# State space phase tables computed for two stages at once, one per half of the partitions

## The chip, the cores and the metric

The kernel runs on one core of a Trainium2 chip. The metric is device time in microseconds of one execution of the whole program, the median of several runs. The program is one decoder layer on 1024 tokens of width 1024, in 32-bit floats.

## The reference, cut to what matters

One layer adds to its input the merged output of three causal token mixers (an attention with forget gates, a diagonal state space, a gated linear recurrence), then a cross attention over 256 memory rows, then a SwiGLU block. The change lies in the state space mixer, with 32 groups of 16 channels and 64 complex states per group:

```
abar = exp(dt * a)                    # a complex, one per group and state
h[t] = abar * h[t-1] + bbar u[t]      # complex, per group and state
y[t] = Re(c h[t]) + d_skip * u[t]
out  = gelu(y) * sigmoid(gelu(y) w_glu + b_glu)
```

The kernel computes the recurrence over chunks of eight tokens: within a chunk by a Toeplitz matrix, from chunk to chunk (128 of them) by a scan. The scan runs on real numbers: each chunk's drive is turned by the angle that the state has moved through up to that chunk, scanned with the magnitude of abar to the eighth power, and turned back. The cosine and sine of these angles, for 128 chunks, are the phases. They depend on the group and the state alone.

## The kernel before, in words

All activations lie transposed, channels on the 128 partitions and tokens along the columns. A 32-bit weight or activation is split into a rounded part and the rest (`wh` and `wl`, `xh` and `xl`): ScalarE writes the first and VectorE the second, by subtraction, and each product is three TensorE matmuls of 128x512 (`pj` groups in PSUM).

The state space mixer is done in eight stages of four groups. A partition pair p and p+64 holds the real and the imaginary part of state p, so the parameters stand twice, once in each half of the partitions, and a sign column `sgn` (-1 below, +1 above) makes the sine's sign differ between the halves. `s5_params` prepares the tables, all with 32 groups along the columns: powers of abar, and two small tables of turned angles, `eb` (16 fine steps) and `ear`, `eai` (8 coarse steps), seeded by GpSimd copies and VectorE scalings and filled by complex products on VectorE.

`s5_main` runs eleven rounds, one stage a round at each of four lags. Round i calls `s5_prep` of stage i (GpSimd products into the tile `s5x`, loads of `s5u`), `s5_out` of stage i-3 (the matmuls `s5y`, which read `kcs`, then the gelu on VectorE and ScalarE in turns, then a store), `s5_prep2` of stage i-1 (the phases, a transposition `s5g`, small matmuls `s5k`, copies on ScalarE, eight DMAs into `toep`), and `s5_body` of stage i-2 (the matmuls `s5d`, multiplication by the phases, four scans, multiplication back, the result in `kcs`). So a stage's phases are computed in the round before its body. They are six VectorE instructions of 128x512: from `ear`, `eai` and `eb` by broadcasting, into the tile `s5e` (cosines in its first 512 columns, signed sines in the second), with a scratch half of `s5tm` between. `toep` and `kcs` have two halves, used in turns by the stage's parity.

Between the stages' calls `pump` places other work for TensorE: the projections of the remaining inputs and gates (`gz`, the value projection `vs` with its weights `w_v`, attention queries and keys `qs`). The Tile framework takes all this in program order with a priority for each instruction, which `ahead` raises (60 for the stages, 60 for weight splits), and fixes each engine's order of instructions at build time by priority and by its own estimate of when an instruction's inputs are ready. On the chip each engine goes through its order and waits on semaphores. Tiles come from one pool of 50 buffers of 128x1024 and 8 PSUM banks; an instruction that first writes a buffer waits for the last readers of what lay there. All DMAs are issued from SyncE's queue.

The names that matter below: `s5_params` (line 898), `s5_prep` (1090), `s5_prep2` (1123), `s5_body` (1171), `s5_out` (1199), `s5_main` (1226). Line 244 is the helper of all two-input element operations, 241 that of ScalarE's activations, 226 that of matmuls, 260 that of scalar operations.

Of the kernel before, what the change touches and what calls it, by code (L numbers as in the profile page):

```python
# [13 lines left out]
AF = mybir.ActivationFunctionType  # L14
# [5 lines left out]
P = 128  # L20
# [50 lines left out]
HG_LAT = 5.0  # L71
FOXL_W = 10.0
FOXL_T = 8.0
EPS = 1e-6
NEG = -1e30
HG_LEVELS = (1, 2, 4, 8, 16)
# [116 lines left out]
class Trunk:  # L193
# [704 lines left out]
    def s5_params(self):  # L898
        nc = self.nc
        V, G = nc.vector, nc.gpsimd  # L900
# [14 lines left out]
        ADD, MUL, SUB = ALU.add, ALU.mult, ALU.subtract  # L915
# [18 lines left out]
        k, r, dt, f2 = tiny(), tiny(), tiny(), tiny()  # L934
# [28 lines left out]
        ang = self.u("s5ang").rearrange("p (q m g) -> p q m g", q=4, m=8)  # L963
# [20 lines left out]
        s, v = ang[:, 2, 0], ang[:, 3, 0]  # L984
        t = tiny()
        yield
        nr, ni, ar1, c = tiny(), tiny(), tiny(), tiny()
# [24 lines left out]
        cx = self.u("s5cx").rearrange("p (a g h) -> p a g h", a=2, h=16)  # L1012
# [23 lines left out]
        tmv = tm.rearrange("p a g h -> p a (g h)")  # L1036
        for n in (1, 2, 4):
            tmp = [tmv[:, i, 0:32 * n].rearrange("p (g k) -> p g k", k=n) for i in range(2)]
# [6 lines left out]
        rv = self.u("s5rv")  # L1045
# [5 lines left out]
        yield  # L1051


        eb = self.u("s5eb").rearrange("p (a g k) -> p a g k", a=2, k=16)
        ear = rv[:, 256:512].rearrange("p (g k) -> p g k", k=8)
        eai = rv[:, 512:768].rearrange("p (g k) -> p g k", k=8)
        for m, j in ((1, 0), (2, 1), (3, 3), (4, 7), (5, 15)):
            G.tensor_copy(out=eb[:, 0, :, j], in_=ang[:, 1, m])
            self.ts(eb[:, 1, :, j], ang[:, 2, m], self.sgn, -1.0, MUL, MUL)
        G.memset(ear[:, :, 0], 1.0)  # L1060
        G.memset(eai[:, :, 0], 0.0)
        for m, j in ((5, 1), (6, 2), (7, 4)):
            G.tensor_copy(out=ear[:, :, j], in_=ang[:, 1, m])
            self.ts(eai[:, :, j], ang[:, 2, m], self.sgn, -1.0, MUL, MUL)

        def fill(tr, ti, first, n, base):
            tmp = [tmv[:, i, 0:32 * n].rearrange("p (g k) -> p g k", k=n) for i in range(2)]
            self.cmul(tr[:, :, base + 1:base + 1 + n], ti[:, :, base + 1:base + 1 + n],
                      tr[:, :, first:first + n], ti[:, :, first:first + n],
                      tr[:, :, base:base + 1].to_broadcast([P, 32, n]),  # L1070
                      ti[:, :, base:base + 1].to_broadcast([P, 32, n]), V, tmp)

        for n in (1, 3, 7):
            fill(eb[:, 0], eb[:, 1], 0, n, n)
# [4 lines left out]
        tz, kz = self.u("toep"), self.u("kcs")  # L1079
# [40 lines left out]
        self.add(Z1, Z1, T, G)  # L1120
        d.update(U=U, ut=ut, xt=xt, X=X, Z1=Z1)

    def s5_prep2(self, o):
        nc = self.nc
        g0 = 4 * o
        gs = slice(g0, g0 + 4)
        d = self.s5o[o]
        ut, xt, X, Z1 = (d[k] for k in ("ut", "xt", "X", "Z1"))
        cx = self.cx

        def bh(t):
            return t[:, gs].unsqueeze(3).to_broadcast([P, 4, 8, 16])

        def bk(t):
            return t[:, gs].unsqueeze(2).to_broadcast([P, 4, 8, 16])


        et = self.u("s5e")
        dt_ = self.u("s5dd")
        CO = et[:, 0:512].rearrange("p (g a j) -> p g a j", g=4, a=8)  # L1140
        SI = et[:, 512:1024].rearrange("p (g a j) -> p g a j", g=4, a=8)
        tq = self.s5t[:, 1].rearrange("p (g a j) -> p g a j", g=4, a=8)
        ar, ai = bh(self.ear), bh(self.eai)
        br, bi = bk(self.eb[:, 0]), bk(self.eb[:, 1])
        self.mul(CO, ar, br)
        self.mul(tq, ai, bi)
        self.sub(CO, CO, tq)
        self.mul(SI, ar, bi)
        self.mul(tq, ai, br)
        self.add(SI, SI, tq)  # L1150

        gp = self.psm("s5g")
        for g in range(4):
            self.tp(gp[:, 128 * g:128 * g + 128], X[:, g].rearrange("p s h -> p (s h)"))

        kp = self.psm("s5k")
        for g in range(4):
            x0 = X[:, g, 7]
            self.mm(kp[0:16, 128 * g:128 * g + 16], x0, cx[:, 0, g0 + g])
            self.mm(kp[0:16, 128 * g + 16:128 * g + 128], x0, Z1[:, g, 0:7].rearrange("p k h -> p (k h)"))  # L1160
        G1 = xt[:, 0:512]
        self.act(G1, gp, AF.Copy)
        kt = ut[0:16, 512:1024]
        self.act(kt, kp[0:16], AF.Copy)
        tz = self.toep[o % 2]
        ktv = kt.rearrange("p (g c) -> p g c", g=4)
        for s in range(8):
            nc.sync.dma_start(out=tz[16 * s:16 * s + 16, :, 16 * s:128], in_=ktv[:, :, 0:128 - 16 * s])
        d.update(et=et, dt=dt_, G1=G1.rearrange("p (g c) -> p g c", g=4), tz=tz)

    def s5_body(self, o):

        d = self.s5o[o]
        U, et, dt_, G1 = (d[k] for k in ("U", "et", "dt", "G1"))
        COf, SIf = et[:, 0:512], et[:, 512:1024]
        d1 = self.psm("s5d1")
        for g in range(4):
            self.mm(d1[:, 128 * g:128 * g + 128], G1[:, g], U[:, g])
        r1, r2 = dt_[:, 0:512], dt_[:, 512:1024]
        lo, hi = slice(0, 64), slice(64, 128)  # L1180
        self.mul(r1, d1, COf)
        self.mul(r2[lo], d1[hi], SIf[hi])
        self.mul(r2[hi], d1[lo], SIf[lo])
        self.sub(r1, r1, r2)
        for g in range(4):
            c = slice(128 * g, 128 * g + 128)
            a = self.r8[:, 4 * o + g:4 * o + g + 1].to_broadcast([P, 128])
            self.nc.vector.tensor_tensor_scan(out=r1[:, c], data0=a, data1=r1[:, c], initial=0.0,
                                              op0=ALU.mult, op1=ALU.add)
        kc = self.kcs[o % 2]  # L1190
        kv = r1.rearrange("p (g c) -> p g c", g=4)
        cv, sv = COf.rearrange("p (g c) -> p g c", g=4), SIf.rearrange("p (g c) -> p g c", g=4)
        m = r2.rearrange("p (g c) -> p g c", g=4)[:, :, 1:128]
        self.mul(kc[:, :, 1:128], kv[:, :, 0:127], cv[:, :, 0:127])
        for a, b in ((lo, hi), (hi, lo)):
            self.mul(m[a], kv[b, :, 0:127], sv[b, :, 0:127])
        self.add(kc[:, :, 1:128], kc[:, :, 1:128], m)

    def s5_out(self, o):

        nc = self.nc
        g0 = 4 * o
        d = self.s5o.pop(o)
        U, ut, Z1, tz = (d[k] for k in ("U", "ut", "Z1", "tz"))
        kc = self.kcs[o % 2]
        yp = self.psm("s5y")
        for g in range(4):
            c = yp[:, 128 * g:128 * g + 128]
# [16 lines left out]

    def s5_main(self):

        self.s5o = {}
        for o in range(11):
            for lag, stage in ((0, self.s5_prep), (3, self.s5_out), (1, self.s5_prep2), (2, self.s5_body)):  # L1230
                if 0 <= o - lag < 8:
                    stage(o - lag)
                    yield S5_W[lag] * (S5_END if o > 8 else S5_BEG if o < 2 else 1.0)
            if o == FOX_AT:
                self.need("ff")
                self.fox_alloc()
# [1083 lines left out]
```

## Time and profile before

| | |
|---|---|
| device time, median of 3 runs | 2147.52 us (2146.33 to 2148.11) |
| the profiled execution, device time | 2145.49 us |
| its span, first to last instruction | 2143.7 us |
| TensorE matmuls busy | 2073.8 us, 97% of the span |
| VectorE busy | 1525.9 us, 71% |
| ScalarE busy | 814.1 us, 38% |
| GpSimd busy | 610.7 us, 28% |

The state space stages lie between about 107 and 322 us of the span. In a profile PE is TensorE, DVE is VectorE, ACT is ScalarE, POOL is GpSimd and SP is SyncE. A row's releaser (after `<-`) is what the idle time ended with. Durations of neighbouring instructions overlap a little, so their sum can be over the elapsed time.

### The profile page before, as it was taken

How to read it: one execution, taken by the hardware profiler on the slowest of the kernel's cores; microseconds unless marked ns; L12 is line 12 of the kernel's file. 1: busy time of each engine (PE TensorE's matmuls, PEld its weight loads, DVE VectorE, ACT ScalarE, POOL GpSimd, SP SyncE). 2: the span in 40 equal slices, each digit the busy share in tenths (PEclk: the TensorE clock that was granted, in tenths of full speed). 3: DMA queues.
4: the chain of work that ended last, by engine and by line, in shares of the span. 5: the costliest groups of instructions: out<-in, count | busy, mean ns of one | idle time of the engine just before them, and what ended most of it. 6: DMA issues, size and time to landing. Idle time of an engine off the chain costs nothing.

```text
span 2143.7 us, 26772 instructions
## 1 busy us (share of the span) xinstructions
PE 2073.8 (97%) x10044; PEld 1701.3 (79%) x10044; DVE 1525.9 (71%) x2221; ACT 814.1 (38%) x1268; POOL 610.7 (28%) x495
## 2 busy tenths in 40 slices
PE   8998999999999999999999999999999999989899
PEld 5887776776788888887888888878788888878677
DVE  8888898889845576536665576756878787866764
ACT  4113355556421222216334455534433333334231
POOL 4281204455531111000603000011432232425740
PEclk9999999999999999999999999999999999999999
DMA  4332120110210121124434533243222232269783
GB/s 162 137 103 75 51 86 21 40 50 30 79 54 30 50 69 55 59 98 171 159 102 144 197 90 108 79 165 125 92 97 102 99 123 98 99 228 356 267 292 132
DMA packets 102610, 245.18 MB, mean 114 GB/s; under 512 B 15816, under 2 KB 32200, under 8 KB 102480
## 3 DMA queue, kind: packets, MB, share of 16 engines
q1 hardware_dynamic: 102480, 243.46, 32.9%
q8 instruction: 79, 1.29, 0.2%
q14 instruction: 51, 0.42, 0.1%
HBM read 184.83 MB, written 57.41 MB: 113 GB/s over the span
## 4 chain that ended last, share of the span: by engine, by line
PE 65%; DVE 4%; issue 1%; DMA 1%; ACT 1%; POOL 1%; SPq 0%; DVEq 0%; POOLq 0%; ACTq 0%
PE pj L226 32%; PE fp L226 26%; PE hs L226 2%; PE xo L226 1%; DVE wc L244 1%; PE rs L226 1%; PE xs L226 1%; DVE hl L244 1%; PE ho L226 1%; POOL t L244 0%; PE hst L226 0%; PE pv L226 0%; PE st L226 0%; DVE tl L244 0%; DMA hr<-hb_d 0%
## 5 line engine op out<-in xcount | busy, mean ns | idle before, releaser
L226 PE MATMUL pj<-xh,wh 128*128 128x512 f32 x784 | 312.8, 404 | 6.7 <-ACT xh L241 5.3
L226 PE MATMUL pj<-xl,wh 128*128 128x512 f32 x784 | 314.1, 404 | 3.5 <-DVE xl L256 3.4
L226 PE MATMUL pj<-xh,wl 128*128 128x512 f32 x784 | 310.4, 399 | 0.0
L226 PE MATMUL fp<-hh,wc 128*128 128x512 f32 x644 | 196.5, 397 | 15.9 <-DVE wc L244 13.2
L226 PE MATMUL fp<-th,wc 128*128 128x512 f32 x640 | 208.2, 391 | 2.2 <-ACT th L241 2.2
L244 DVE TENSOR_TENSOR wl<-wr,wh 128x1024 fp32r<-128x1024 f32 (+2 forms) x138 | 166.1, 1204 | 52.1 <-ACT wh L241 50.2
L226 PEld LDWEIGHTS pj<-xh,wh 128*128 128x128 f32 x784 | 148.9, 190 | 39.6 <-ACT xh L241 5.8
L226 PEld LDWEIGHTS pj<-xl,wh 128*128 128x128 f32 x784 | 148.0, 189 | 35.4 <-DVE xl L256 5.8
L226 PE MATMUL fp<-fx,wc 128*128 128x512 f32 x720 | 173.0, 389 | 0.0
L226 PEld LDWEIGHTS pj<-xh,wl 128*128 128x128 f32 x784 | 148.4, 189 | 30.7 <-issue 2.2
L241 ACT ACTIVATE wh<-wr 128x1024 fp32r<-128x1024 f32 (+2 forms) x138 | 131.6, 957 | 76.6 <-DMA wr<-w_in 39.6
L226 PEld LDWEIGHTS fp<-hh,wc 128*128 128x128 f32 x644 | 123.1, 192 | 44.7 <-DVE wc L244 15.8
L226 PEld LDWEIGHTS fp<-fx,wc 128*128 128x128 f32 x720 | 135.2, 188 | 28.1
L244 DVE TENSOR_TENSOR wc<-wr,wc 128x512 fp32r<-128x512 f32 (+1 forms) x116 | 119.7, 1054 | 40.9 <-ACT wc L241 40.9
L226 PEld LDWEIGHTS fp<-th,wc 128*128 128x128 f32 x640 | 120.9, 189 | 27.8 <-ACT th L241 2.7
L244 POOL TENSOR_TENSOR acc<-acc,sq 128x512 f32<-128x512 f32 (+1 forms) x18 | 30.8, 1709 | 375.5 <-ACT sq L241 375.4
L226 PE MATMUL fp<-tl,wc 128*128 128x512 f32 x320 | 125.3, 392 | 1.6 <-DVE tl L244 1.6
L244 DVE TENSOR_TENSOR pt<-pf,pt 128x512 fp32r<-128x512 f32 (+1 forms) x96 | 94.1, 983 | 39.6 <-POOL pt L260 39.3
L244 POOL TENSOR_TENSOR fc<-fc,fs 128x512 f32<-128x512 f32 x40 | 57.3, 1433 | 220.3 <-ACT fs L241 220.3
L226 PE MATMUL fp<-hl,wc 128*128 128x512 f32 x280 | 111.1, 397 | 0.0
L260 POOL TENSOR_SCALAR pt<-pf 128x512 fp32r<-128x512 f32 (+1 forms) x96 | 68.8, 717 | 136.4 <-ACT pf L241 126.0
L241 ACT ACTIVATE wc<-wr 128x512 fp32r<-128x512 f32 (+1 forms) x116 | 76.9, 699 | 64.4 <-POOL wr L244 47.4
(429 smaller groups left out, 4841.2 us busy)
## 6 DMA issues: line engine op xcount, KB each, us to landing
wr<-w_in SPq DMA_DIRECT2D x48, 512.0 KB, 4.1
wr<-w_gu SPq DMA_DIRECT2D x44, 512.0 KB, 4.1
wr<-w_dn SPq DMA_DIRECT2D x36, 512.0 KB, 7.1
hr<-hb_d SPq DMA_DIRECT2D x35, 512.0 KB, 6.7
hb_d<-fc SPq DMA_DIRECT2D x44, 256.0 KB, 2.1
gz_d<-gz SPq DMA_DIRECT2D x20, 512.0 KB, 2.9
gate<-gz_d SPq DMA_DIRECT2D x20, 512.0 KB, 3.7
wr<-xo SPq DMA_DIRECT2D x17, 512.0 KB, 4.9
```

The lines of the kernel that those rows point to most:

```text
L226: self.nc.tensor.matmul(out, lhsT, rhs, start=start, stop=stop)
L241: self.nc.scalar.activation(out=out, in_=in_, func=f, **kw)
L244: return (eng or self.nc.vector).tensor_tensor(out=out, in0=a, in1=b, op=op)
L260: (eng or self.nc.vector).tensor_scalar(out=out, in0=a, scalar1=s1, scalar2=s2, op0=op0, **kw)
```

## The change

The small tables `eb`, `ear` and `eai` get 16 groups along the columns instead of 32: the lower half of the partitions holds groups 0 to 15, the upper half groups 16 to 31. Each seed is written by two instructions, one per half; each filling has half the columns. The six phase instructions then give the phases of stage o (groups 4o to 4o+3) in the lower half and of stage o+4 in the upper half. Five ScalarE copies of 64 partitions make two full tiles of them, `et` for stage o and `e2` for stage o+4, with the sines' sign turned where they change halves. The stages run in the order 0, 4, 1, 5, 2, 6, 3, 7, so that both stages of a pair follow each other, and the phases are computed in the first one's `s5_prep2` alone. The halves of `toep` and `kcs` go by the place in that order.

```diff
+S5_SEQ = (0, 4, 1, 5, 2, 6, 3, 7)
...
-        eb = self.u("s5eb").rearrange("p (a g k) -> p a g k", a=2, k=16)
-        ear = rv[:, 256:512].rearrange("p (g k) -> p g k", k=8)
-        eai = rv[:, 512:768].rearrange("p (g k) -> p g k", k=8)
+        eb = self.u("s5eb")[:, 0:512].rearrange("p (a g k) -> p a g k", a=2, k=16)
+        ear = rv[:, 256:384].rearrange("p (g k) -> p g k", k=8)
+        eai = rv[:, 512:640].rearrange("p (g k) -> p g k", k=8)
+        halves = ((slice(0, 64), slice(0, 16)), (slice(64, 128), slice(16, 32)))
+
+        def seed(tr, ti, m, j):
+            for h, g in halves:
+                G.tensor_copy(out=tr[h, :, j], in_=ang[h, 1, m, g])
+                self.ts(ti[h, :, j], ang[h, 2, m, g], self.sgn[h], -1.0, MUL, MUL)
+
         for m, j in ((1, 0), (2, 1), (3, 3), (4, 7), (5, 15)):
-            G.tensor_copy(out=eb[:, 0, :, j], in_=ang[:, 1, m])
-            self.ts(eb[:, 1, :, j], ang[:, 2, m], self.sgn, -1.0, MUL, MUL)
+            seed(eb[:, 0], eb[:, 1], m, j)
...
         def fill(tr, ti, first, n, base):
-            tmp = [tmv[:, i, 0:32 * n].rearrange("p (g k) -> p g k", k=n) for i in range(2)]
+            tmp = [tmv[:, i, 0:16 * n].rearrange("p (g k) -> p g k", k=n) for i in range(2)]
...
-    def s5_prep2(self, o):
...
+    def s5_phases(self, o):
...
-        et = self.u("s5e")
-        dt_ = self.u("s5dd")
+        et, e2 = self.u("s5e"), self.u("s5e")
...
         self.mul(SI, ar, bi)
         self.mul(tq, ai, br)
         self.add(SI, SI, tq)
+        lo, hi = slice(0, 64), slice(64, 128)
+        c, s = slice(0, 512), slice(512, 1024)
+        self.act(e2[hi], et[hi], AF.Copy)
+        self.act(e2[lo, c], et[hi, c], AF.Copy)
+        self.act(e2[lo, s], et[hi, s], AF.Copy, scale=-1.0)
+        self.act(et[hi, c], et[lo, c], AF.Copy)
+        self.act(et[hi, s], et[lo, s], AF.Copy, scale=-1.0)
+        self.s5ph[o], self.s5ph[o + 4] = et, e2
+
+    def s5_prep2(self, o):
...
+        if o < 4:
+            self.s5_phases(o)
+        et = self.s5ph.pop(o)
+        dt_ = self.u("s5dd")
...
-        tz = self.toep[o % 2]
+        tz = self.toep[S5_SEQ.index(o) % 2]
...
-        kc = self.kcs[o % 2]
+        kc = self.kcs[S5_SEQ.index(o) % 2]
...
-                    stage(o - lag)
+                    stage(S5_SEQ[o - lag])
```

## Rows read from the trace of the kernel before

**Rows 1.** The page's first part: each engine's busy time, share of the span and instructions.

```profile
PE 2073.8 (97%) x10044; PEld 1701.3 (79%) x10044; DVE 1525.9 (71%) x2221; ACT 814.1 (38%) x1268; POOL 610.7 (28%) x495
```

**Rows 2.** Busy times of the engines by stretch, over the four stretches of the state space stages. Columns: the stretch, its length, then busy time (and instructions) of PE, PEld, DVE, ACT and POOL, the granted TensorE clock as a share of full speed, the DMA engines' share and GB/s.

```profile
107.20:160.80 53.60, 53.53 (x289) 44.30 (x288) 47.37 (x52) 9.66 (x13) 43.57 (x30) 1.00 0.33 103
160.80:214.40 53.60, 46.30 (x242) 37.85 (x242) 43.07 (x65) 17.13 (x23) 8.61 (x6) 0.97 0.26 75
214.40:268.00 53.60, 51.63 (x271) 41.62 (x269) 46.49 (x82) 16.32 (x29) 15.05 (x11) 1.00 0.20 51
268.00:321.60 53.60, 51.12 (x266) 41.46 (x267) 50.81 (x89) 26.89 (x35) 2.13 (x3) 1.00 0.29 86
```

**Rows 3.** The waits of PE between 0 and 450 us: who waited for whom, us in total, times, the longest.

```profile
PE s5y L226 <- DVE kcs L244: 10.4, 7, 3.3
...
PE pj L226 <- DVE wl L244: 1.3, 2, 1.0
```

**Rows 4.** The timeline of PE in short stretches, around each stage's matmuls `s5y` that read `kcs`. Columns: start, us, engine, line, operation, tiles, forms and number; in brackets the idle time before it and its releaser.

```profile
148.82 0.38 PE L226 MATMUL s5y<-kcs,s5x 128*128 128x128 f32 x2
...
150.30 0.48 PE L226 MATMUL pj<-xh,wh 128*128 128x512 f32 x1
...
169.10 0.49 PE L226 MATMUL s5y<-kcs,s5x 128*128 128x128 f32 x2 [2.61 <-DVE kcs L244]
...
205.60 0.80 PE L226 MATMUL s5y<-kcs,s5x 128*128 128x128 f32 x2 [3.34 <-DVE kcs L244]
...
208.61 0.51 PE L226 MATMUL pj<-wl,xh 128*128 128x512 f32 x1
...
222.39 0.38 PE L226 MATMUL s5y<-kcs,s5x 128*128 128x128 f32 x1 [0.30 <-DVE kcs L244]
...
247.74 0.38 PE L226 MATMUL s5y<-kcs,s5x 128*128 128x128 f32 x1 [1.33 <-DVE kcs L244]
...
268.55 0.38 PE L226 MATMUL s5y<-kcs,s5x 128*128 128x128 f32 x1 [0.89 <-DVE kcs L244]
...
292.26 0.38 PE L226 MATMUL s5y<-kcs,s5x 128*128 128x128 f32 x1 [1.22 <-DVE kcs L244]
...
310.29 0.38 PE L226 MATMUL s5y<-kcs,s5x 128*128 128x128 f32 x1 [0.71 <-DVE kcs L244]
```

**Rows 5.** Busy times by stretch around the wait at 205.60, columns as in Rows 2.

```profile
202.30:205.60 3.30, 0.00 (x1) 0.00 (x1) 3.24 (x7) 1.68 (x4) 0.00 (x0) 0.95 0.00 0
205.60:209.00 3.40, 3.40 (x16) 3.36 (x17) 1.80 (x5) 0.00 (x0) 0.00 (x0) 0.55 0.00 0
```

**Rows 6.** The timeline of DVE in three stretches, each from a stage's phases (`s5e` from `s5rv` and `s5eb`) to the body of the stage before (`s5dd` from `s5d` and `s5e`). Columns as in Rows 4.

```profile
187.24 1.28 DVE L244 TENSOR_TENSOR s5e<-s5rv,s5eb 128x512 f32<-128x512 f32 x2
...
191.05 0.68 DVE L244 TENSOR_TENSOR s5e<-s5e,s5tm 128x512 f32<-128x512 f32 x1
191.65 2.09 DVE L244 TENSOR_TENSOR s5dd<-s5d,s5e 128x512 f32<-128x512 f32 x3
193.77 2.24 DVE L244 TENSOR_TENSOR wl<-wr,wh 128x1024 fp32r<-128x1024 f32 x1
...
233.94 1.29 DVE L244 TENSOR_TENSOR s5e<-s5rv,s5eb 128x512 f32<-128x512 f32 x2 [4.11 <-PE pj L226]
...
237.74 2.08 DVE L244 TENSOR_TENSOR s5dd<-s5d,s5e 128x512 f32<-128x512 f32 x3
...
274.95 1.29 DVE L244 TENSOR_TENSOR s5e<-s5rv,s5eb 128x512 f32<-128x512 f32 x2
...
279.35 0.68 DVE L244 TENSOR_TENSOR s5dd<-s5d,s5e 128x512 f32<-128x512 f32 x1
```

**Rows 7.** Groups of DVE's instructions between 106 and 322 us, shapes kept apart: the split of weights and the three groups that are the phases. Columns: line, engine, operation, tiles, forms and number; busy us, mean ns of one; idle us before them and releasers.

```profile
L244 DVE TENSOR_TENSOR wl<-wr,wh 128x1024 fp32r<-128x1024 f32 x15 | 21.0, 1402 | 1.3 <-ACT wh L241 1.2
L244 DVE TENSOR_TENSOR s5tm<-s5rv,s5eb 128x512 f32<-128x512 f32 x16 | 16.9, 1059 | 0.2
L244 DVE TENSOR_TENSOR s5e<-s5e,s5tm 128x512 f32<-128x512 f32 x16 | 15.0, 938 | 0.1
L244 DVE TENSOR_TENSOR s5e<-s5rv,s5eb 128x512 f32<-128x512 f32 x16 | 14.0, 910 | 4.1 <-PE pj L226 4.1
```

**Rows 8.** Groups of ACT's instructions between 92 and 322 us, columns as in Rows 7.

```profile
L241 ACT ACTIVATE k<-qs 64x1024 fp32r<-64x1024 f32 x3 | 3.2, 1054 | 3.6 <-DVE qs L256 3.5
...
L241 ACT ACTIVATE qmm<-qs 64x512 fp32r<-64x512 f32 x3 | 1.9, 632 | 1.7 <-PE mx L226 1.6
```

**Rows 9.** The tile `s5eb` between 93 and 107 us: instructions that write or read it, with min, median and max ns, first and last start, and forms.

```profile
L244 DVE TENSOR_TENSOR s5tm<-s5eb x9: 225/383/1528, 94.9 to 103.6; 128x32 f32<-128x32 f32 x3, 128x96 f32<-128x96 f32 x3, 128x224 f32<-128x224 f32 x3
...
L260 DVE TENSOR_SCALAR s5eb<-s5ang,cst x5: 263/1792/2028, 94.2 to 94.8; 128x32 f32<-128x32 f32 x5
```

**Rows 10.** The waits of DVE and of POOL between 90 and 330 us, columns as in Rows 3. Both instructions are first writers of a buffer.

```profile
DVE s5e L244 <- PE pj L226: 4.1, 1, 4.1
...
POOL s5x L244 <- DVE wl L244: 33.9, 1, 33.9
```

**Rows 11.** The stores to and the first loads from the scratch tensor `su_d`, columns as in Rows 9, and over all su stores the time to landing.

```profile
L1100 SPq DMA_DIRECT2D s5u<-su_d x8: 302/424/1232, 93.5 to 98.4; - x8
L884 SPq DMA_DIRECT2D su_d<-su x4: 319/326/330, 48.2 to 71.5; - x4
...
DMA to landing us min/median/max: 2.6/2.9/7.1
```

More of the change, by code (lines that the diff above doesn't have):

```diff
@@ L1062, in s5_params @@
         for m, j in ((5, 1), (6, 2), (7, 4)):
-            G.tensor_copy(out=ear[:, :, j], in_=ang[:, 1, m])
-            self.ts(eai[:, :, j], ang[:, 2, m], self.sgn, -1.0, MUL, MUL)
+            seed(ear, eai, m, j)
         def fill(tr, ti, first, n, base):
-            tmp = [tmv[:, i, 0:32 * n].rearrange("p (g k) -> p g k", k=n) for i in range(2)]
+            tmp = [tmv[:, i, 0:16 * n].rearrange("p (g k) -> p g k", k=n) for i in range(2)]
             self.cmul(tr[:, :, base + 1:base + 1 + n], ti[:, :, base + 1:base + 1 + n],
                       tr[:, :, first:first + n], ti[:, :, first:first + n],
-                      tr[:, :, base:base + 1].to_broadcast([P, 32, n]),
-                      ti[:, :, base:base + 1].to_broadcast([P, 32, n]), V, tmp)
+                      tr[:, :, base:base + 1].to_broadcast([P, 16, n]),
+                      ti[:, :, base:base + 1].to_broadcast([P, 16, n]), V, tmp)
         for n in (1, 3, 7):
@@ L1121, in s5_prep @@
         d.update(U=U, ut=ut, xt=xt, X=X, Z1=Z1)
-    def s5_prep2(self, o):
[L1124 to L1129, printed above, removed]
+    def s5_phases(self, o):
+        gs = slice(4 * o, 4 * o + 4)
         def bh(t):
@@ L1150, in s5_prep2 @@
         self.add(SI, SI, tq)
+        lo, hi = slice(0, 64), slice(64, 128)
[7 more added lines that the diff above has]
+    def s5_prep2(self, o):
+        nc = self.nc
+        g0 = 4 * o
+        d = self.s5o[o]
+        ut, xt, X, Z1 = (d[k] for k in ("ut", "xt", "X", "Z1"))
+        cx = self.cx
+        if o < 4:
+            self.s5_phases(o)
+        et = self.s5ph.pop(o)
+        dt_ = self.u("s5dd")
         gp = self.psm("s5g")
@@ L1204, in s5_out @@
         U, ut, Z1, tz = (d[k] for k in ("U", "ut", "Z1", "tz"))
-        kc = self.kcs[o % 2]
+        kc = self.kcs[S5_SEQ.index(o) % 2]
         yp = self.psm("s5y")
@@ L1226, in s5_main @@
     def s5_main(self):
-        self.s5o = {}
+        self.s5o, self.s5ph = {}, {}
         for o in range(11):
```

## The prediction

> **What bounds the kernel now.** I read the page's busy shares first: TensorE is busy 97% of the span [rows 1], so a change can only pay where TensorE stands idle, and can only cost where it makes TensorE idle. Then the busy times by stretch, over the four stretches that hold the state space stages [rows 2]: TensorE is busy 53.5, 46.3, 51.6 and 51.1 us of some 53.6 each, together 11.8 us idle, while VectorE is busy 47.4, 43.1, 46.5 and 50.8 us. VectorE is the second fullest engine here, and nearly full in the last stretch. Next, who TensorE waited for [rows 3]: 10.4 us in seven waits for the result that a stage's body leaves in kcs, 1.3 us for split weights (wl). That is nearly the whole idle time of these stretches, so the most that this change can win at its own place is these 11.7 us and what the clock adds. The seven waits one by one, in TensorE's order of time [rows 4], show where they stand. I number the stages by their place, P0 to P7: P0 has no wait, then P1 2.61 us, P2 3.34, P3 0.30, P4 1.33, P5 0.89, P6 1.22, P7 0.71. After the wait of P2 the granted clock is 0.55 over the next 3.4 us, against 0.95 to 1.00 before [rows 5], that is, nearly all of it at 1.2 of 2.4 GHz: the seven groups of s5y take 3.01 us there (205.60 to 208.61) and 1.48 us at P0 (148.82 to 150.30) [rows 4]. That wait costs 3.34 + 1.5 us.
>
> **What is removed.** A stage's phases are six VectorE instructions of 128x512, 48 in all, 16.9 + 15.0 + 14.0 = 45.9 us [rows 7]. The change keeps those of P0, P2, P4 and P6, and drops the 24 of P1, P3, P5 and P7: at least 24 x 0.68 = 16.3 us [rows 6], 23.0 us at the mean of 0.96 [rows 7]. This is VectorE time; what it is worth to TensorE is read from VectorE's order [rows 6]. A stage's phases stand one round ahead of its own body, right in front of the body of the stage before: those of P3 run from 187.24 to 191.7, and the body of P2 starts at 191.65; those of P5 start at 233.94, the body of P4 at 237.74; those of P7 at 274.95, the body of P6 at 279.35. So the dropped groups are just those ahead of the bodies on which the waits of P2, P4 and P6 hang, five instructions or 3.4 us in front of each: more than each of the three waits (3.34, 1.33, 1.22, together 5.9 us), and for P4 also an idle 4.11 us of VectorE ahead of its first phase instruction.
>
> If TensorE kept its order, these 5.9 us and the 1.5 us of clock would go: 7.4 us. It will not keep it. The s5y groups stand in the middle of projection groups [rows 4], where the framework's scheduler put them at build time, when by its estimate kcs is ready; with less VectorE work it puts them earlier too. What a wait then measures is how far the chip's VectorE runs behind that estimate. Some of the lag stays: the wl split at 193.77 takes 2.24 us where the mean of its group is 1.40 [rows 6, 7], and it is not touched. Bounds: nothing to 5.9 us, and nothing to 1.5 us of clock. I take half of each, 2.9 + 0.8 = 3.7 us, as no row is nearer to one end. The 1.3 us for wl lie in the same crowd as P2 (0 to 1.3; I take nothing, since the waits stand at weights whose ScalarE half the change does not speed), and the 4.5 us of P1, P3, P5 and P7 have kept phases ahead of them: nothing, bounds 0 to 4.5.
>
> **What is added.** Per pair five ScalarE copies on 64 partitions: one of 1024 columns and four of 512. The nearest rows are the same forms, 1.05 us and 0.63 us [rows 8]: half of the partitions does not make them cheaper. 1.05 + 4 x 0.63 = 3.6 us a pair, 14.3 us in all. ScalarE is busy 17.1, 16.3 and 26.9 us in the last three stretches [rows 2], so there is room. Their results are due a round later, some 20 us (bodies of P4 and P6 are 41.6 us apart, two rounds [rows 6]). The added wait: the first copy waits for VectorE's last addition, and holds what is queued on ScalarE behind it: weight halves (wh, for which wl and then TensorE wait), evacuations of the value projection (vs) and the squares of the stage ahead. Cover is that idle time of ScalarE; without it a pair costs up to 3.6 us on TensorE. Bounds 0 to 14.3 us, no gain; I take nothing for the copies.
>
> **What moves.** The setup's seeds become 16 VectorE instructions for 8 and 16 GpSimd copies for 8, and its 30 table fillings halve their columns. VectorE's seeds range from 0.26 to 2.03 us, its fillings around 0.38 [rows 9]: the eight added seeds cost 2 us at the short end and 16 at the long one, the halved fillings give back 1 to 3. TensorE is busy 53.53 of 53.6 us behind it [rows 2] with projections, so I take nothing; without that cover it is up to 15 us, but no wait on it is seen there. The order 0, 4, 1, 5, ... needs the third su block at the second stage instead of the fifth: the last su store is issued at 71.5 and the first load of a stage at 93.5 [rows 11], so this costs nothing; without that slack it would be one landing, 2.6 to 7.1 us. The DMAs of a stage are as many as before, and pass no other on SP's queue. Each second table e2 lives a round longer than the table it replaces: 4 x 20 us over 215 us, 0.4 of 50 buffers on average. Buffers are short: VectorE waited 4.1 us with an s5e write until TensorE had read what lay there, GpSimd 33.9 us with s5x [rows 10]. One such wait more costs VectorE up to 4.1 us; bounds 0 to 4.1 for each of four, I take 0.2 us.
>
> The sum is 3.7 - 0.2 = 3.5 us. The profiled execution took 2145.49 us, 2143.7 of span and 1.8 around it, 2.0 below the median of the runs. Against it the sum gives 2142.0; against the median of 2147.5, **2144.0 us**.
>
> **The rivals.** *A, the forecast*: waits of P2, P4 and P6 shrink in part, 2141.5 to 2146.5. *B, the crowd is gone*: the three waits, the clock's dip and the wl waits all vanish, 5.9 + 1.5 + 1.3 = 8.7 us, 2138.8. For it: five instructions stand directly ahead of each body. Against it: the scheduler moves s5y along.
>
> *C, nothing comes through*: TensorE stays as full as it is, the idle ones trade places, 2147.5. For it: in the stretch where the phases are dearest, from 107 to 160, TensorE has no idle time to give back [rows 2]. The Trainium skill (Perfetto Trace Analysis, Identifying the Most-Contended Engine) says that the engine with the highest occupancy is to be improved first; by that rule a relief of VectorE is worth nothing here. The trace does not bear it out in full: the named waits of 10.4 us end with VectorE [rows 3]. That it doesn't do what it says would look like C too: 24 phase instructions fewer must be seen.
>
> *D, slower, by ScalarE's queue*: its place is where the value projection runs, 185 to 250, in which weights come fast enough that TensorE already waits for wl and kcs. If the copies of the pairs computed at P2 and P4 hold back wh or vs there, each costs 3.6 us on TensorE and, as after the wait of P2, a dip of the clock of 1.5 us: 2 x 5.1 = 10.2, less the 3.5 of A, 2154.2. It makes the kernel slower from the point where the copies cost TensorE more than those 3.5 us, that is, where one pair is exposed in full. Against it: ScalarE is idle two thirds of that time.
>
> **How the numbers follow.** A 0.40, B 0.24, C 0.16, D 0.20. About 0.2%, 4.3 us, is what a measurement of this kernel can tell from no change. B is beyond that, and of A the part below 2143.2, which I put at 0.14: faster 0.38. The rest of A and C: same 0.42. D: slower 0.20. The range reaches into B, to 2137, which also takes some of the 4.5 us of P1, P3, P5 and P7, and to D's 2154; A's own range stands above.
>
> **What would show it.** VectorE's phase groups at 8 instructions each for 16, some 16 to 23 us less; 20 new ScalarE copies of 0.63 and 1.05 us; the waits of s5y for kcs at P2, P4 and P6 below 3 us together and the clock's dip gone or smaller; no new wait of TensorE on wl, xl or a PSUM buffer. Wrong would be: waits for kcs as long as before (C), or a wait for wh, wl or vs with copies ahead of it on ScalarE (D), or the time moving outside 107 to 330, which no step here foresees.

## The result, and the profile after

The changed kernel takes 2164.59 us (median of 7 runs, 2161.93 to 2168.88) against 2148.29 us (7 runs, 2146.33 to 2157.05) on the same chip: a ratio of 1.0072, 95% interval 1.0055 to 1.0089. It is slower by 16 us, outside the predicted range of 2137 to 2154. The profiled execution has a span of 2162.8 us against 2143.7, and a mean granted clock of 0.989 against 0.994.

The page's first part of the kernel after, which answers to [rows 1], and the busy times by stretch, which answer to [rows 2] with the same columns:

```profile
PE 2084.0 (96%) x10044; PEld 1709.5 (79%) x10044; DVE 1508.1 (70%) x2205; ACT 828.5 (38%) x1288; POOL 613.0 (28%) x503
```

```profile
107.20:160.80 53.60, 53.54 (x289) 44.24 (x288) 34.28 (x42) 12.11 (x17) 40.64 (x30) 1.00 0.35 111
160.80:214.40 53.60, 44.57 (x223) 36.37 (x222) 37.26 (x56) 19.42 (x28) 8.04 (x6) 0.90 0.25 73
214.40:268.00 53.60, 51.35 (x265) 41.93 (x264) 35.10 (x63) 19.71 (x33) 13.32 (x11) 0.97 0.18 42
268.00:321.60 53.60, 46.26 (x222) 37.16 (x221) 45.44 (x76) 29.79 (x39) 1.89 (x2) 0.94 0.20 61
```

VectorE is emptier in every stretch, 152.1 us busy in the four against 187.7, and TensorE is emptier too: idle 0.06 + 9.03 + 2.25 + 7.34 = 18.7 us, before 11.8. Its clock is lower: as a share of full speed the shortfall is (0.10 + 0.03 + 0.06) x 53.6 = 10.2 us, before 0.03 x 53.6 = 1.6. Idle time and clock together are 6.9 + 8.6 = 15.5 us of the 19.1 by which the two spans differ. By 321.6 us TensorE has started 999 instructions in these stretches instead of 1068. So some four fifths of the loss arise here, where the change is. Most of the rest are two more falls of the clock behind them: 0.89 from 520 to 535 us and 0.91 from 2060 to 2080, where the kernel before has 1.00 (520 to 535, and 2040 to 2060), together some 3.5 us.

The change did what it says. Groups of VectorE between 106 and 322 us, which answer to [rows 7]: eight phase instructions for sixteen, 8.2 + 7.1 + 7.0 = 22.3 us for 45.9.

```profile
L245 DVE TENSOR_TENSOR s5e<-s5e,s5tm 128x512 f32<-128x512 f32 x8 | 8.2, 1024 | 0.1
L245 DVE TENSOR_TENSOR s5e<-s5rv,s5eb 128x512 f32<-128x512 f32 x8 | 7.1, 922 | 0.0
L245 DVE TENSOR_TENSOR s5tm<-s5rv,s5eb 128x512 f32<-128x512 f32 x8 | 7.0, 874 | 0.2
...
L245 DVE TENSOR_TENSOR s5dd<-s5d,s5e 128x512 f32<-128x512 f32 x8 | 5.5, 685 | 10.4 <-DMA sz_d<-s5u 5.0 <-PE pj L227 3.3 <-PE s5d L227 2.1
```

The last of these rows is the first product of a stage's body: idle for 0.0 us ahead of it in the kernel before, now 10.4 us, of which 5.0 + 3.3 us end with a store and with projection matmuls, neither of which is part of this body: readers, as I take it, of what lay in the buffer that it is given.

ScalarE's copies, in the same window, cost what was reckoned, 0.63 and 1.06 us, 13.9 us in all:

```profile
L242 ACT ACTIVATE s5e<-s5e 64x512 f32<-64x512 f32 x16 | 9.7, 628 | 10.2 <-DVE s5e L245 10.0
...
L242 ACT ACTIVATE s5e<-s5e 64x1024 f32<-64x1024 f32 x4 | 4.2, 1060 | 3.3 <-DVE s5e L245 3.3
```

The waits of PE between 100 and 345 us, which answer to [rows 3], and the single waits in PE's timeline, which answer to [rows 4]:

```profile
PE s5y L227 <- DVE kcs L245: 13.5, 6, 3.7
PE pj L227 <- ACT wh L242: 2.8, 1, 2.8
PE rs L227 <- ACT sq L242: 2.7, 1, 2.7
```

```profile
171.40 0.58 PE L227 MATMUL s5y<-kcs,s5x 128*128 128x128 f32 x1 [2.35 <-DVE kcs L245]
...
194.67 0.51 PE L227 MATMUL pj<-wh,xh 128*128 128x512 f32 x1 [2.77 <-ACT wh L242]
...
209.16 0.58 PE L227 MATMUL s5y<-kcs,s5x 128*128 128x128 f32 x1 [3.59 <-DVE kcs L245]
...
252.07 0.38 PE L227 MATMUL s5y<-kcs,s5x 128*128 128x128 f32 x1 [2.25 <-DVE kcs L245]
...
283.92 0.58 PE L227 MATMUL s5y<-kcs,s5x 128*128 128x128 f32 x1 [3.74 <-DVE kcs L245]
...
290.88 1.22 PE L227 MATMUL rs<-sq,cst 128*128 128x512 f32 x1 [2.73 <-ACT sq L242]
...
306.72 0.38 PE L227 MATMUL s5y<-kcs,s5x 128*128 128x128 f32 x1 [0.87 <-DVE kcs L245]
```

The three waits that were to shrink are not gone: P2 3.59 (before 3.34), P4 2.25 (1.33), P6 0.87 (1.22). P5 has grown from 0.89 to 3.74. Two waits of 2.8 and 2.7 us for ScalarE are new. Two places can be followed in VectorE's timeline, whose counterpart is [rows 6]. At P2:

```profile
194.65 1.22 DVE L245 TENSOR_TENSOR wl<-wr,wh 128x1024 fp32r<-128x1024 f32 x1 [5.77 <-ACT wh L242]
195.80 2.09 DVE L245 TENSOR_TENSOR s5dd<-s5d,s5e 128x512 f32<-128x512 f32 x3
```

The phases of P3 no longer stand ahead of this body, and yet it starts 4.15 us later than before (195.80 against 191.65): in their place VectorE is idle for a weight half. ScalarE's timeline says why that half is late, and SP's where the load stood. First ScalarE after and before, then SP after and before:

```profile
193.56 1.06 ACT L242 ACTIVATE wh<-wr 128x1024 fp32r<-128x1024 f32 x1 [5.94 <-DMA wr<-w_v]
```

```profile
188.81 2.25 ACT L241 ACTIVATE wh<-wr 128x1024 fp32r<-128x1024 f32 x2 [2.74 <-DMA wr<-w_v]
```

```profile
180.20 3.58 SPq L1242 DMA_DIRECT2D sz_d<-s5u  x8
183.90 5.06 SPq L1187 DMA_DIRECT2D toep<-s5u  x8
189.00 1.06 SPq L347 DMA_DIRECT2D wr<-w_v  x2
```

```profile
175.36 3.58 SPq L1223 DMA_DIRECT2D sz_d<-s5u  x8
179.57 5.05 SPq L1168 DMA_DIRECT2D toep<-s5u  x8
184.66 1.06 SPq L346 DMA_DIRECT2D wr<-w_v  x2
```

On SP's queue (SPq) stand, in both kernels, the stores of P1's output (sz_d), then eight toep transfers, then loads of the value projection's weights. P1's s5y began 2.3 us later (171.40 against 169.10): counted from P1's first s5d, 62 projection matmuls stand ahead of it in TensorE's order, before 52, and ten of them take about 2.3 us. Then it ran at half of the clock. Its output was stored 4.84 us later, the load was issued 4.34 us later, and the weight half came 4.75 us later, just ahead of the body of P2.

At P5, with the phases of P6 in front of it as before:

```profile
270.56 0.69 DVE L245 TENSOR_TENSOR s5e<-s5e,s5tm 128x512 f32<-128x512 f32 x1
274.56 2.10 DVE L245 TENSOR_TENSOR s5dd<-s5d,s5e 128x512 f32<-128x512 f32 x3 [3.30 <-PE pj L227]
```

The body stands 3.30 us in a wait for projection matmuls; TensorE's wait of 3.74 us for its kcs ends 9.4 us after the body's start.

### The profile page after: what moved, and what is told of

It is laid out like the page before. It is cut to its first block, busy times and chain, and to the rows that moved or that the text cites. A ratio compares the mean times of both kernels' runs of the same rounds, so it can differ in the third digit from the quotient of the medians.

```text
span 2162.8 us, 26798 instructions
## 1 busy us (share of the span) xinstructions
PE 2084.0 (96%) x10044; PEld 1709.5 (79%) x10044; DVE 1508.1 (70%) x2205; ACT 828.5 (38%) x1288; POOL 613.0 (28%) x503
## 4 chain that ended last, share of the span: by engine, by line
PE 63%; DVE 4%; DMA 2%; issue 1%; ACT 1%; POOL 1%; SPq 0%; DVEq 0%; POOLq 0%; ACTq 0%
PE pj L227 31%; PE fp L227 25%; PE hs L227 2%; DMA hr<-hb_d 2%; DVE wc L245 1%; PE xo L227 1%; PE xs L227 1%; PE rs L227 1%; PE ho L227 1%; DVE hl L245 1%; POOL t L245 0%; PE hst L227 0%; PE pv L227 0%; DMA wr<-xv 0%; PE st L227 0%
## 5 line engine op out<-in xcount | busy, mean ns | idle before, releaser
L227 PE MATMUL fp<-hh,wc 128*128 128x512 f32 x644 | 197.8, 399 | 16.2 <-DVE wc L245 13.5
```

Of the source, the lines that this page charges most:

```text
L227: self.nc.tensor.matmul(out, lhsT, rhs, start=start, stop=stop)
```

## The experiments

Three causes were in question: ScalarE's copies and what they hold up in its queue (Q in the texts on record, the cause of rival D), the buffer that each second table e2 holds for two rounds (B), and the relief of VectorE itself. The texts on record also weigh O, the new order by itself, and call the framework's scheduler the planner. Each ratio is to the kernel before on the same chip, with its 95% interval.

**Copies alone, order alone.** To the kernel before were added, after the phases of every second stage, five ScalarE copies of the change's shapes, in place:

```
         self.add(SI, SI, tq)
+        if o % 2 == 0:
+            lo, hi = slice(0, 64), slice(64, 128)
+            c, s = slice(0, 512), slice(512, 1024)
+            self.act(et[hi], et[hi], AF.Copy)
+            for h, w in ((lo, c), (lo, s), (hi, c), (hi, s)):
+                self.act(et[h, w], et[h, w], AF.Copy)
```

> The kernel before, in its own order, every stage with its own phases; after the phases of each even stage five ScalarE copies of the same shapes as the change's, in place, so that the body waits for them as in the change. The values are the same. VectorE keeps all 48 phase instructions. Theory Q: 2158 to 2168, most of the 16 us, with waits of TensorE on wh or sq that end with ScalarE. Theory B: 2148 to 2151, as no buffer is added. Theory O: no forecast by itself, anywhere from 2145 to 2165.

Measured: 1.0004 (0.9991 to 1.0017). TensorE waits for kcs 10.8 us in 7 waits, before 10.4 in 7. Copies of this number and size cost nothing while VectorE is as full as before; `skip_odd_copies` below has them with VectorE relieved. The other run took only S5_SEQ and the three indices by it:

> The kernel before with only the stages' order changed to 0, 4, 1, 5, 2, 6, 3, 7: every stage computes its own phases, no ScalarE copies, no second tile. Theory B (one more buffer held for a round takes buffers from the body's tile and from loads, and the waits grow): 2148, within 3 us of before, since no buffer is added. Theory Q (the five ScalarE copies hold back what is queued behind them on ScalarE): 2148 as well, since there are no copies. Theory O (any new build-time order places s5y and the loads anew and costs about this much by itself): 2155 to 2170.

Measured: 1.0006 (0.9997 to 1.0015). The order of the stages costs nothing.

**One buffer alone.** To the kernel before was added a tile of e2's size that a one-column copy opens where the change opens e2, and that a one-column operation at the end of the next stage's body reads for the last time:

```
+        if o % 2 == 0:
+            self.s5hold = self.u("s5e")
+            self.act(self.s5hold[:, 0:1], et[:, 0:1], AF.Copy)
...
+        if o % 2:
+            self.ts(r1[:, 0:1], self.s5held, 1.0)
+            self.s5held = None
+        else:
+            self.s5held, self.s5hold = self.s5hold[:, 0:1], None
```

> The kernel before, in its own order; each even stage also takes one more buffer when its phases are done and keeps it until the next stage's body is done, as the change's e2 is kept (one column copied into it by ScalarE, read once by VectorE at the end). Theory B: 2156 to 2168, with first writers of buffers (s5dd, s5x, wr) waiting longer, and weights arriving late. Theory Q: 2148 to 2150. Theory O: anywhere from 2145 to 2165.

Measured: 2177.69 us, 1.0139 (1.0122 to 1.0156): 29 us for a buffer with next to no work in it. Waits of PE, and of VectorE, between 100 and 345 us, and the place in VectorE's and in PE's timeline:

```profile
PE s5y L226 <- DVE kcs L244: 21.6, 5, 5.9
...
DVE s5dd L244 <- PE pj L226: 16.2, 1, 16.2
```

```profile
238.37 2.09 DVE L244 TENSOR_TENSOR s5dd<-s5d,s5e 128x512 f32<-128x512 f32 x3 [16.20 <-PE pj L226]
```

```profile
250.64 0.79 PE L226 MATMUL s5y<-kcs,s5x 128*128 128x128 f32 x2 [4.37 <-DVE kcs L244]
```

The wait is of the kind seen at P5 of the change, and larger: the body's first product waits 16.2 us for projections, which read, as I take it, what lies in its buffer, and s5y waits.

But more is held here than in the change. There e2 stands in for the odd stage's own table; here the tile is held beside both tables. By the order of the calls, where one pair meets the next, two tables are in use at once in the kernel before, three in the change, and four buffers here; between these places it is two, two and three. The trace shows the overlap: the second tile is opened at 158.74 and last read at 250.50, and the third is opened at 231.45.

```profile
158.74 0.20 ACT L241 ACTIVATE s5e<-s5e 128x1 f32<-128x1 f32 x1 [4.29 <-DVE s5e L244]
...
231.45 0.19 ACT L241 ACTIVATE s5e<-s5e 128x1 f32<-128x1 f32 x1
```

```profile
250.50 0.14 DVE L260 TENSOR_SCALAR s5dd<-s5e 128x1 f32<-128x1 f32 x1
```

So the 29 us show that this pool has no buffer to spare; they are not the price of e2.

**A buffer given back.** In the changed kernel the half tables take less room, so all of them fit into free parts of rv and pw, and s5eb needs no buffer. `packed` builds them there; `packed_late` builds them as the change does and lets GpSimd move them there when they are finished:

```
+        keep = rv[:, 512:1024].rearrange("p (a g k) -> p a g k", a=2, k=16)
+        eai2 = rv[:, 384:512].rearrange("p (g k) -> p g k", k=8)
+        G.tensor_copy(out=eai2, in_=eai)
+        G.tensor_copy(out=keep, in_=eb)
+        self.ear, self.eai, self.eb = ear, eai2, keep
...
-        self.s5d, self.r8 = rv[:, 768:800], rv[:, 800:832]
+        self.s5d, self.r8 = pw[:, 832:864], pw[:, 864:896]
```

> The changed kernel with the fine table eb packed into the free half of the tile that holds the coarse ones, so that the buffer s5eb is given back: the change's e2 then takes no more buffers than before had. Copies, order and phases as in the change. Theory B: most of the 16 us come back, 2145 to 2153. Theory Q: 2162 to 2168, as the copies are the same. Theory O: anywhere from 2145 to 2170.

> The changed kernel, with eb and eai copied by two GpSimd instructions at the end of the setup into free parts of the tile of the coarse tables, so that the buffer s5eb is given back only when the stages begin, and the setup is the change's. TensorE's build-time order is that of packed. If the change's loss is a part for the buffer and a part for s5y moved forward by less VectorE work (as skip_odd showed it, 5 us): 2152 to 2157, 5 to 10 us of the 16 back, the rest as in skip_odd. If the buffer doesn't matter in the changed kernel: 2163 or more.

Measured: 1.0051 (1.0034 to 1.0068) and 1.0042 (1.0029 to 1.0055). In packed_late about 6 of the 16 us come back, and 9 us stay, so e2's buffer is a cause and not the only one. The evidence is not strong: packed_late's interval just meets the change's (1.0055 to 1.0089), and packed's overlaps it. The waits of PE in packed_late:

```profile
PE s5y L227 <- DVE kcs L245: 9.4, 5, 3.7
PE pj L227 <- ACT wh L242: 2.9, 1, 2.9
```

**The relief alone.** The kernel before, with the phases of every second stage left out. Those stages use the table of the stage ahead of them, which is kept a round longer in place of their own; no e2, no copies. By the order of the calls this also leaves one buffer free in every second round, one table in use for two, so the relief does not come quite alone:

```
-        et = self.u("s5e")
+        if o % 2 == 0:
+            self.s5et = self.u("s5e")
+        et = self.s5et
...
+        if o % 2 == 0:
...
+        if o % 2:
+            self.s5et = None
```

> The kernel before, with the phases of the odd stages left out: each odd stage reads the tile of the even stage before it, kept one round longer instead of a tile of its own (so the odd stages turn by the wrong angles). 24 phase instructions of VectorE fewer, no copies, no more buffers than before. This is the gain by itself. The prediction's step: 2144, 3.7 us faster, with the waits of P2, P4 and P6 about halved. If a relief of VectorE is worth nothing here (rival C): 2148. If the planner answers less VectorE work with longer waits of TensorE: 2152 or more.

Measured: 2155.13 us against 2149.55, 1.0023 (1.0012 to 1.0034). VectorE does 24 instructions less, and the kernel is about 5 us slower. That goes with a lower clock: its ten runs have mean granted clocks of 0.988 to 0.991 and take 2151.7 to 2157.6 us; of the nineteen runs of the kernel before on that chip the three at 0.989 and 0.990 take 2152.7 to 2154.8 us, and the others, at 0.991 to 0.994, 2145.3 to 2151.4. The waits of PE for kcs, and two of them in its timeline:

```profile
PE s5y L226 <- DVE kcs L244: 10.2, 6, 3.7
```

```profile
202.24 0.38 PE L226 MATMUL s5y<-kcs,s5x 128*128 128x128 f32 x1 [1.35 <-DVE kcs L244]
...
244.56 0.80 PE L226 MATMUL s5y<-kcs,s5x 128*128 128x128 f32 x2 [3.71 <-DVE kcs L244]
```

The waits sum to 10.2 us, before 10.4: P2 shrank from 3.34 to 1.35, P4 grew from 1.33 to 3.71 (of the others P1 lost its 2.61, and P0 has a new one of 1.86). How far TensorE moved its s5y can be counted. The busy times of the tile pj alone, at P4 from its first s5d to its first s5y that reads kcs, of the kernels before, after and skip_odd; the PEld column counts the projection matmuls between the two by their weight loads:

```profile
231.50:247.74 16.24, 14.26 (x61) 10.93 (x59) 2.51 (x6) 2.53 (x6) 1.00 0.26 70
```

```profile
234.40:252.07 17.67, 13.21 (x56) 10.18 (x55) 3.64 (x8) 3.22 (x8) 1.00 0.14 31
```

```profile
228.50:244.56 16.06, 11.48 (x50) 8.95 (x48) 2.78 (x6) 2.41 (x6) 0.96 0.24 64
```

59, 55 and 48. At 14.26 / 61 = 0.234 us for one, skip_odd's s5y stands 11 x 0.234 = 2.6 us further forward, and its wait is 2.38 us longer; the change's stands 4 x 0.234 = 0.9 forward, and its wait is 0.92 longer. At P4 nearly the whole move turns into waiting. Counted so at all eight places, skip_odd's s5y stands 6, 4, 11, 4 and 7 further forward at P2 to P6 and is unmoved at P0, P1 and P7. In the change it stands 6, 4 and 11 further forward at P2, P4 and P6, the three whose waits were to shrink, and 8, 10, 26 and 22 further back at P0, P1, P3 and P5.

**The change without its relief.** The changed setup, half tables, order and ScalarE copies, but each stage computes its own six instructions into a table of its own, completed by two 64x512 copies; there is no e2:

```
-        gs = slice(4 * o, 4 * o + 4)
+        gs = slice(4 * (o % 4), 4 * (o % 4) + 4)
...
-        et, e2 = self.u("s5e"), self.u("s5e")
+        et = self.u("s5e")
...
+        d, f = (hi, lo) if o < 4 else (lo, hi)
+        self.act(et[d, c], et[f, c], AF.Copy)
+        self.act(et[d, s], et[f, s], AF.Copy, scale=-1.0)
...
-        if o < 4:
-            self.s5_phases(o)
+        self.s5_phases(o)
```

> The change's half tables, order and ScalarE copies, but every stage computes its phases itself (six VectorE instructions as before) into one tile and has it completed by two copies of 64x512; no second tile. Theory B (the buffer that e2 holds): 2147 to 2150, since nothing of the change that holds a buffer is left. If half tables, setup or copies cost: 2153 or more.

Measured: 1.0007 (0.9995 to 1.0020), and 10.7 us of waits for kcs. The matmuls between s5d and s5y are as many as in the kernel before at all eight places (59, 52, 82, 120, 59, 41, 53, 59). So setup, half tables, copies and order cost nothing together either, and s5y does not move in them.

**The order within a round.** In both kernels the body was called ahead of the phases and the input products of the stage behind it:

```
-            for lag, stage in ((0, self.s5_prep), (3, self.s5_out), (1, self.s5_prep2), (2, self.s5_body)):
+            for lag, stage in ((0, self.s5_prep), (3, self.s5_out), (2, self.s5_body), (1, self.s5_prep2)):
```

> The changed kernel with the body of a stage called ahead of the next phases in each round, instead of behind them: the odd stage's e2 is then free before the next pair's two tiles are taken, so that two of these tiles are held at the most, as before, and not three. Theory B: 2146 to 2156, most of the loss back. If the loss sits in the copies' wait for VectorE: no better, 2162 or more.

> The kernel before with the same swap, body ahead of the next stage's phases. By the prediction's reading of VectorE's order the phases no longer stand between s5d and kcs, so the waits of s5y for kcs shrink by up to half of their 10.4 us: 2141 to 2146. Theory B: one tile less is held at the peak, so no worse than before. If the planner moves s5y along: 2148.

Measured: after_swap 1.0078 (1.0055 to 1.0101), no better than the change; before_swap 1.0079 (1.0048 to 1.0110). The buffer theory of the first text and the prediction's reading in the second both missed. A body that comes earlier by its place in the program makes no kernel faster. Beside before_swap the change costs nothing (1.0078 for 1.0079, each known to about 0.3%): in this order no loss by the change is seen, and why was not followed.

**TensorE asked later.** If s5y stands too far forward, it may be put back: the s5y matmuls were given a priority 150 places later, in three kernels.

```
+            self.ahead(-150, lambda: (
-            self.mm(c, tz[:, g], U[:, g], True, False)
-            self.mm(c, Z1[:, g].rearrange("p k h -> p (k h)"), kc[:, g], False, True)
+                self.mm(c, tz[:, g], U[:, g], True, False),
+                self.mm(c, Z1[:, g].rearrange("p k h -> p (k h)"), kc[:, g], False, True)))
```

> The kernel before, with the matmuls s5y given a lower priority (150 places later), which moves the first that reads kcs behind 20, 31, 14, 25, 18, 25, 9 and 24 more projection matmuls at P0 to P7. If the waits for kcs are a matter of where the planner puts s5y: each place is 0.227 us, more than each of the waits but little more at P2 and P6, so the 10.4 us nearly go, and the clock's dip at P2 with them: 2137 to 2141. If the delay goes round (gelu, store and the weight loads behind it on SyncE's queue later): 2146 to 2152.

> The changed kernel with the same lower priority for s5y. If the placing of s5y explains the loss but for the buffer: 2145 to 2153. If the buffer alone explains it: 2160 or more.

> packed_late with the same lower priority for s5y: 24 phase instructions fewer, no buffer more, s5y late. If both parts of the explanation hold, the waits for kcs go and the relief of VectorE costs nothing: 2136 to 2143, about the same as or below the kernel before with the later s5y. If something else of the change costs: 2148 or more.

Measured: 1.0211 (1.0196 to 1.0226), 1.0162 (1.0147 to 1.0177), 1.0171 (1.0156 to 1.0186): all far slower. Waits of PE in before_s5y150 between 90 and 400 us:

```profile
PE pj L226 <- ACT wh L241: 5.4, 2, 5.0
PE pv L226 <- POOL pt L260: 5.4, 2, 4.4
...
PE s5y L226 <- DVE kcs L244: 0.5, 1, 0.5
```

The wait for kcs is nearly gone, 0.5 us of 10.4, and others of more than that have come. That a later s5y delays its output's store, and with it the loads queued behind it, would explain the waits for wh; it was not followed here.

**Does the sum close?** Relief and held buffer together, relief and copies together, and a buffer more for the change without relief:

> skip_odd (24 phase instructions left out, odd stages turn by the wrong angles) with one more buffer taken when an even stage's phases are done and kept until the next stage's body, as in hold_buffer. If the change's loss is the relief (5 us, skip_odd) and the buffer of e2: 2162 to 2175, at least as slow as the change. If the buffer costs only where VectorE is full (hold_buffer kept all 48 phase instructions): 2153 to 2158.

> skip_odd with the five ScalarE copies in place after the phases of each even stage, no second tile: the relief and the copies without the buffer. If the 4 us by which packed_late stays behind skip_odd are the copies, which cost nothing as long as VectorE is as full as before (copies_only): 2157 to 2161. If they are not: 2153 to 2156, as skip_odd.

> own_phases (every stage computes its phases itself, with half tables and two copies) with the tables moved at the end of the setup as in packed_late, so that the stages have one buffer more than in the kernel before. If buffers set the pace here: below before, 2138 to 2146, with VectorE's wait of 4.1 us for an s5e buffer gone. If the kernel before has enough of them: 2147 to 2152, as own_phases.

Measured: skip_odd_hold 1.0078 (1.0062 to 1.0094), beside the change's 1.0072; skip_odd_copies 1.0015 (1.0002 to 1.0029), no more than skip_odd; own_packed 1.0020 (1.0001 to 1.0038). Relief and a held buffer make a loss of the change's size, without a copy between partitions. They do not make it in the same way: where pairs meet, skip_odd_hold has four buffers in use and the change three, and its largest wait of VectorE is 17.4 us, where the change has 5.0 and 3.3. The waits of PE and of VectorE in skip_odd_hold (L260 in the first is the added read, 0.15 us long, with which two waits for a body end):

```profile
PE s5y L226 <- DVE kcs L244: 10.5, 4, 4.9
PE s5y L226 <- DVE s5dd L260: 8.6, 2, 4.4
...
DVE s5dd L244 <- PE pj L226: 17.4, 1, 17.4
```

The change without its relief has as many buffers as the kernel before; one more than that brings it nothing (own_packed). It moves s5y forward all the same: at P4 51 projection matmuls stand ahead of it, not 59, and its wait is 3.09 us, not 1.33, though all 48 phases are computed. At P2 it is unmoved (82, as before; skip_odd 76).

```profile
232.10:248.32 16.22, 12.48 (x53) 9.44 (x51) 1.90 (x4) 1.79 (x4) 0.98 0.39 104
```

```profile
248.32 0.58 PE L227 MATMUL s5y<-kcs,s5x 128*128 128x128 f32 x1 [3.09 <-DVE kcs L245]
```

So a free buffer moves s5y too, and as skip_odd has one in every second round, its move at P4 is not shown to come from VectorE's relief alone. None of these kernels is faster than the one before.

## Why the prediction was wrong

**What bounds the kernel** was read rightly in one thing: most of what happened, 15.5 of 19.1 us, shows in TensorE's idle time and clock of the four stretches (two falls of the clock, 3.5 us, came behind them). Read wrongly was what a wait of TensorE is worth: "the most that this change can win" took the waits, 10.4 us for kcs and 1.3 for wl, for time that a faster VectorE gives back.

**What is removed: the step that failed first.** 24 instructions went as reckoned, 23.6 us where 16 to 23 stood. The value taken, 3.7 us (2.9 of waits, 0.8 of clock), was wrong: skip_odd, the relief without e2 and copies, gains nothing and loses 0.23%, about 5 us. The prediction named the reason for less, "the scheduler moves s5y along". The counts show that this ate the gain: at P2 of skip_odd the wait shrank by 2.0 us, at P4 the move turned into waiting nearly in full, and the sum of the waits stayed (10.2 for 10.4). The loss on top of that goes with a lower granted clock and not with longer waiting, and for the clock the sum had only a gain: in the change the clock cost 8.6 us in the four stretches. That s5y moved is counted. That the scheduler's estimate of kcs moved it is argued: it moves forward at P2, P4 and P6 in the change and in skip_odd and nowhere in own_phases, but own_packed moves it at P4 without any relief. The rule weighed under rival C, of the Trainium skill (Perfetto Trace Analysis, Identifying the Most-Contended Engine), that the engine with the highest occupancy is to be improved first, fits skip_odd in so far as 24 VectorE instructions fewer gained nothing; that it cost 0.23% the rule does not say.

**What moves, buffers: the term that was mis-sized.** "0.4 of 50 buffers on average", "I take 0.2 us". Giving one buffer back returns 0.0072 - 0.0042, or 6 us (packed_late): thirty times what was taken, though inside the bounds of 0 to 4.1 us for each of four. Holding more than the change does costs more: 29 us in the kernel before (hold_buffer) and, on top of the relief, 0.0078 - 0.0023, or 12 us (skip_odd_hold). The average was the wrong measure: what counts is whether a buffer is free when a body asks for one, and the body's first write waited 16.2 us at 238.37 in hold_buffer, and 5.0 and 3.30 us in the change. [Rows 10] already showed such waits, and the bound of 4.1 us each was taken from the shorter of the two.

**What is added, setup, order: right.** Copies at 0 (copies_only; skip_odd_copies is no slower than skip_odd), order at 0 (order_only), setup with half tables at 0 (own_phases). ScalarE's copies cost the 14 us of ScalarE time that were named, all of it beside other work.

**Rival D** foretold the direction, less than half of the loss (2154.2), and the signs at their place: waits for wh, a dip of the clock, between 185 and 250. Its cause is refuted by copies_only and own_phases. The wh was late not behind copies but behind its own load, which stood on SP's queue behind P1's store. So the point that D named, "where the copies cost TensorE more than those 3.5 us", was not reached, and the kernel became slower without it.

**What stays open.** skip_odd's waits in the four stretches are no longer than before, and TensorE's idle time there is 11.7 us, before 11.8; of the 10.3 us by which its span is longer than that of the kernel before (2154.0 and 2143.7 us, the latter one of that kernel's fastest executions) the clock there accounts for some 3 (0.94 and 0.97 in the last two stretches, 0.09 x 53.6 = 4.8, where before it fell short by 1.6). A further stretch far behind, with TensorE busy throughout, has a lower clock in it, worth 0.13 x 40 = 5.2 us; skip_odd first, then before:

```profile
760.00:800.00 40.00, 40.00 (x211) 31.36 (x211) 24.68 (x36) 9.48 (x11) 5.83 (x5) 0.87 0.23 82
```

```profile
760.00:800.00 40.00, 40.00 (x233) 31.28 (x232) 27.34 (x38) 10.26 (x13) 8.64 (x6) 1.00 0.23 79
```

Why it is lower there was not found. It does not come with the relief every time: the same stretch has 0.87 in packed_late and 1.00 in the change and in skip_odd_copies, which leaves out the same 24 instructions. Nor is it settled why the held tile costs 29 us in the kernel before and 12 on top of the relief, where between the pairs two buffers are in use and not three, and what makes the 4 us between packed_late (1.0042) and skip_odd (1.0023); the intervals of these two just overlap, and packed_late still has the wait of 2.9 us for wh.

## What to carry to other kernels

A wait of TensorE on a nearly full helper, in a kernel whose order is fixed at build time, need be no stock of time to be won: cut the helper's work, and the waiting instruction can move forward as well, in the order made at build time, and wait as long as before. Count the instructions between two fixed points of TensorE's order to see it. Before a change that saves work by keeping a result longer, look for first writers that wait on a buffer's old readers; if there are any, price one more buffer by a run that holds one with nothing in it, which is a few lines, and not by its share of the pool; and hold it where and as long as the change will, since here a tile held longer cost 29 us where the change's own buffer cost about 6.

## What the runs showed of the hardware

The length of a wait did not tell whether the granted clock fell behind it. Before, P1's wait of 2.61 us is followed by a clock of 1.00; in the change one of 2.35 us at the same place is followed by 0.54, that is, nearly all at 1.2 of 2.4 GHz. Busy times from the start of that s5y, before and after:

```profile
169.10:172.50 3.40, 3.40 (x22) 3.12 (x23) 1.67 (x5) 0.38 (x1) 0.00 (x0) 1.00 0.36 141
```

```profile
171.40:174.80 3.40, 3.40 (x16) 3.36 (x17) 0.58 (x2) 0.00 (x0) 0.00 (x0) 0.54 0.45 171
```

The same stretch holds 16 matmuls instead of 22. Before, of the seven waits for kcs only that of P2 is followed by such a fall; in the change six waits between 170 and 295 us are (for kcs at P1, P2, P4 and P5, for wh and for the squares), and by the count over the four stretches the clock (8.6 us) took more from the change than the waiting itself (6.9 us).
